# The attention loop of a hybrid encoder layer: single operations at written-down places instead of the automatic order

## Chip, cores and metric

The kernel runs on one core of one Trainium2 chip. The metric is the device time of one launch in microseconds (us), the median of the runs shown below. TensorE is called PE here, VectorE DVE, ScalarE ACT, GpSimd POOL and SyncE SP, as in the profile.

## What is computed

One encoder layer over 1024 rows of width 1024, in float32. The part that matters here is the windowed attention, the output projection behind it, and the router of the expert layer:

```
proj  = layer_norm(x) @ w_in                      # split into retention, S5 and attention columns
scores = q . k - slope * |t - s|                  # 8 heads, 2 key heads; a block of 128 rows sees 3 blocks of keys
m     = max(max(scores), sink)
p     = exp(scores - m);  denom = sum(p) + exp(sink - m)
y_att = (p / denom) @ v
mix   = concat(y_ret, y_ssm, y_att) @ w_out
h     = LN(alpha * h + mix)
aff   = softmax(h @ router_w)                     # 16 experts; each takes its 128 best rows
h     = LN(alpha * h + experts(h))                # SwiGLU, 16 experts of 1024 x 2048
```

## The kernel before

The 1024 rows are cut into 8 tiles of 128 rows (NT = 8, the last is LT = 7). The program has three stages. The first (`front`, up to about 284 us) makes the projections, the retention and S5 parts, and the scores of the first tile. The second, the attention loop (284 to about 460 us), is what the change is about; it ends in `last_tile`, which ranks the rows for the first expert. The third stage runs the experts, and lasts until 1604 us.

Most float32 products are made from a high part and a low part, each held in a type with a shorter mantissa: ACT copies the high part, DVE subtracts it from the value to get the low part, and PE multiplies the pairs (`mm3` issues three matmuls: L64, L65, L66 in the profile). So most tiles come as `xh`/`xl`, or as `[:, 0]` and `[:, 1]`.

The loop runs over i = 2 * tile + key head, 16 turns, and calls for each turn, with offsets between them:

- `attention_queries` (L1299): POOL starts the transfer of the queries of one turn, tile `qs`, three buffers.
- `attention_scores`: per head two matmuls into `at` (L1337, L1338), then one DVE instruction (L1341) that adds the bias, writes the scores `S` and gives the row maximum. Behind the four heads, two small DVE instructions (L1346, L1347).
- `attention_exp`: ACT takes exp of the four heads and their sums (L1357, L1359).
- `attention_out`: DVE adds and inverts the sums (L1369, L1370); ACT scales the four heads (L1372); for each of the 3 key blocks PE transposes four 128x128 blocks into `tp` (L1378), ACT and DVE split them into `pT` (L55, L56), and PE multiplies by the values into `po` (L1385). Then ACT and DVE split the result into rows of `yh`, `yl` (L55, L56, L1391).
- `out_proj_load`: the transfer of the old rows `z`, and the split of the retention and S5 rows into `yh`, `yl` (L55, L56).
- `out_proj_part`: 24 matmuls for one half of the columns (L64, L65, L66 into `mm`), then DVE adds them into `z` (L1425) and takes statistics (L1428). `out_proj_stats` finishes the statistics (L1436, L1438 on DVE, L1439 on POOL).
- `router`: PE transposes the new rows (L1478), ACT copies them (`rt`, L1480), PE multiplies by the router's weights (L1490), DVE and ACT make the softmax (`affinities`, L1498 to L1507); DVE normalizes `z` (L1512, L1517); SP stores the rows, ACT scales them, SP stores them again.
- `token_parts` (POOL) and `rank_tile`: a transpose of one column (L1610), ACT's copy (L1635), and DVE's counts (L1618, L1621; for tiles 2 and 5 also L1629).

Each engine works through one list of instructions in order. In `front` and `last_tile` the lists are written by hand (`tc.manual_schedule`). In the loop they are not: it stands outside of any such block, and a scheduler with a timeline of its own picks the order of the single instructions on each engine. Its order may mix the instructions of several calls and turns.

Of the kernel before, what the change touches and what calls it, by code (L numbers as in the profile page):

```python
# [945 lines left out]
def front(K, I, pool, close):  # L946
# [158 lines left out]
    def states_space():  # L1105
        close(X["c_s5a"], X["c_work"])
        X["ast"] = pool("ast")
        K.ast = X["ast"][1]
        X["s5v"] = pool("s5v")
        K.s5v = X["s5v"][1]  # L1110
        K.VS = K.s5v.tile([P, 2, 16, 16, 8], F32, name="VS")
        K.qscale = K.ast.tile([P, 4], F32, name="qscale")
        for u in range(4):
            for b in range(2):
                nc.gpsimd.memset(K.qscale[b * 64:(b + 1) * 64, u:u + 1], 2.0 ** (2 * u + b + 1) / 8.0)
        X["lags"] = Lags(K, I)
        level(K.ast, 160)
# [157 lines left out]
    for g, i, g0 in ((2.7, 0, 0), (9.5, 0, 2), (11.4, 1, 0), (13.5, 1, 2)):  # L1275
        at(A + g, lambda i=i, g0=g0: attention_scores(K, i, g0, g0 + 2))
# [3 lines left out]
    for g, i, g0 in ((10.4, 0, 0), (13.7, 0, 2), (15.65, 1, 0), (17.35, 1, 2)):  # L1280
        at(A + g, lambda i=i, g0=g0: attention_exp(K, i, g0, g0 + 2))
# [20 lines left out]
def attention_space(K):  # L1302
# [3 lines left out]
    K.heads = 0  # L1306
# [15 lines left out]
def attention_scores(K, i, g0=0, g1=4):  # L1322

    nc = K.nc
    c, kv = divmod(i, 2)
    b0, b1 = max(c - 1, 0), min(c + 2, NT)
    W, ro, k0 = (b1 - b0) * P, (b0 - c + 1) * P, b0 * P
    if g0 == 0:
        K.P[i] = [], K.small.tile([P, 5, 4], F32, name="asm", bufs=3)
    S, sm = K.P[i]  # L1330
    qs = K.Q[i]
    m, nm, rs, es, rd = (sm[:, k] for k in range(5))
    hs = slice(kv * 4, kv * 4 + 4)
    for g in range(g0, g1):
        h = kv * 4 + g
        ps = K.pat.tile([P, 512], F32, name="at")
        nc.tensor.matmul(ps[:, :W], qs[:, g, :], K.KHL[kv][:, 0, k0:k0 + W], start=True, stop=False)  # L1337
        nc.tensor.matmul(ps[:, :W], qs[:, g, :], K.KHL[kv][:, 1, k0:k0 + W], start=False, stop=True)  # L1338
        s = K.score[K.heads % 10]
        K.heads += 1  # L1340
        nc.vector.tensor_tensor_reduce(s[:, :W], ps[:, :W], K.R[:, ro:ro + W], 2.0 ** -(h + 1),  # L1341
                                       K.sink[:, h:h + 1], OP.add, OP.max, accum_out=m[:, g:g + 1])
        S.append(s)
    if g1 == 4:
        K.Q.pop(i)
        nc.vector.tensor_scalar(nm, m, -1.0, None, op0=OP.mult)  # L1346
        nc.vector.tensor_tensor(es, K.sink[:, hs], m, OP.subtract)  # L1347


def attention_exp(K, i, g0=0, g1=4):  # L1350
    nc = K.nc
    c = i // 2
    W = (min(c + 2, NT) - max(c - 1, 0)) * P
    S, sm = K.P[i]
    m, nm, rs, es, rd = (sm[:, k] for k in range(5))
    if g0 == 0:
        nc.scalar.activation(es, es, AF.Exp)  # L1357
    for g in range(g0, g1):
        nc.scalar.activation(S[g][:, :W], S[g][:, :W], AF.Exp, bias=nm[:, g:g + 1], accum_out=rs[:, g:g + 1])  # L1359


def attention_out(K, i):
    nc = K.nc
    c, kv = divmod(i, 2)
    b0, b1 = max(c - 1, 0), min(c + 2, NT)
    W = (b1 - b0) * P
    S, sm = K.P.pop(i)
    m, nm, rs, es, rd = (sm[:, k] for k in range(5))
    nc.vector.tensor_tensor(rd, rs, es, OP.add)  # L1369
    nc.vector.reciprocal(rd, rd)  # L1370
    for g in range(4):
        nc.scalar.activation(S[g][:, :W], S[g][:, :W], AF.Copy, scale=rd[:, g:g + 1])  # L1372
    po = K.po.tile([P, 512], F32, name="po")
    pTs = []
    for b in range(b0, b1):
        pt = K.ptp.tile([P, 4, P], F32, name="tp")
        for g in range(4):
            nc.tensor.transpose(pt[:, g, :], S[g][:, (b - b0) * P:(b - b0 + 1) * P], K.ident)  # L1378
        pT = K.ast.tile([P, 2, 512], F32R, name="pT", tag="k4", bufs=3)
        split(K, pT[:, 0], pT[:, 1], pt.rearrange("p a b -> p (a b)"))  # L1380
        pTs.append(pT)
    for b in range(b0, b1):
        pT = pTs[b - b0]
        for s in range(2):
            nc.tensor.matmul(po, K.AV[:, b, kv].rearrange("p s c -> p (s c)"), pT[:, s], start=(b == b0 and s == 0),  # L1385
                             stop=(b == b1 - 1 and s == 1))
    yh, yl, _ = K.Y[c]
    r = slice(kv * 64, (kv + 1) * 64)
    hi, lo = (po[i * 64:(i + 1) * 64].rearrange("p (a b) -> p a b", a=4) for i in range(2))
    split(K, yh[r, 4:8, :], yl[r, 4:8, :], hi)  # L1390
    nc.vector.tensor_tensor(yl[r, 4:8, :], lo, yl[r, 4:8, :].bitcast(F32), OP.add)  # L1391
# [8 lines left out]
def out_proj_load(K, t):  # L1400
    nc, pool, y = K.nc, K.op, K.y.pop(t)
    z = pool.tile([P, D], F32, name="z", bufs=3)
    rows = nc.sync.dma_start(z, K.h_dram[t])
    yh = K.opy.tile([P, KC, P], F32R, name="yh", bufs=2)
    yl = K.opy.tile([P, KC, P], F32R, name="yl", bufs=2)
    split(K, yh[:, 0:2, :], yl[:, 0:2, :], y)
    split(K, yh[:, 2:4, :], yl[:, 2:4, :], K.YO[:, :, t * 16:(t + 1) * 16, :].rearrange("p m k i -> p m (k i)"))
    K.Y[t] = yh, yl, z
    if t + 2 < NT:
        out_proj_rows(K, t + 2)  # L1410
    return rows


def out_proj_part(K, t, n, c0=0, c1=KC):

    nc = K.nc
    yh, yl, z = K.Y[t]
    ns = slice(n * 512, (n + 1) * 512)
    if c0 == 0:
        K.ps = K.pmm.tile([P, 512], F32, name="mm")  # L1420
    for c in range(c0, c1):
        mm3(nc, K.ps, (yh[:, c], yl[:, c]), [K.WO[s][c // 4][:, c % 4, ns] for s in range(2)], c == 0, c == KC - 1)
    if c1 < KC:
        return
    nc.vector.scalar_tensor_tensor(z[:, ns], z[:, ns], ALPHA, K.ps, op0=OP.mult, op1=OP.add)  # L1425
# [67 lines left out]
def affinities(K, t):  # L1493
# [13 lines left out]
    nc.vector.tensor_scalar(K.aff[:, t, :], a, s[:, 2:3], None, op0=OP.mult)  # L1507
# [12 lines left out]
def out_proj_store(K, t):  # L1520

    nc, z = K.nc, K.Y[t][2]
    nc.sync.dma_start(K.h1_dram[t * P:(t + 1) * P, :], z)
    late = t >= NT - 2
    ah = K.op.tile([P, D], F32, name="ah", tag="z" if late else "rt", bufs=3 if late else 1)
    nc.scalar.activation(ah, z, AF.Copy, scale=ALPHA)
    nc.sync.dma_start(K.acc_dram[t * P:(t + 1) * P, :], ah)


def router(K, t):  # L1530

    for q in range(2):
        router_turn(K, t, q)
    for q in range(2):
        router_part(K, t, q)
    affinities(K, t)
    out_proj_gain(K, t)
    out_proj_shift(K, t)
    out_proj_store(K, t)

# [72 lines left out]

def rank_before(K, row, t, col, own):
# [18 lines left out]
def rank_tile(K, t):  # L1633
    own = K.rows[:, t * P:(t + 1) * P]
    K.nc.scalar.activation(own, rank_row(K, K.aff[:, t, 0:1]), AF.Copy)  # L1635
    G = rank_before(K, K.rows[:, 0:(t + 1) * P], t, 0, own)
# [6 lines left out]
    return G  # L1643

# [398 lines left out]
def last_tile(K, I, O, pool, close):  # L2043

    nc, X, t = K.nc, K.X, LT - 1
    for q in range(2):
        router_turn(K, t, q)
# [6 lines left out]
    out_proj_store(K, t)  # L2054
# [33 lines left out]
    out_proj_store(K, LT)  # L2088
# [149 lines left out]
def build(tc, nc, I, O):  # L2238
# [55 lines left out]
    K.P, K.Y = {}, {}  # L2294
# [3 lines left out]
    K.mr, K.st, K.pr = {}, {}, {}  # L2298
    ahead = 2
# [133 lines left out]
```

## Time and profile before

| what | value |
|---|---|
| median of 3 runs | 1606.16 us (1604.99 to 1610.3) |
| the profiled execution | 1606.46 us, of it 1604.7 us in the span |
| granted PE clock over the span | 0.998 |
| busy: PE, DVE, ACT, POOL | 1560.3, 1404.2, 1118.0, 191.8 us |
| first transpose of the loop (L1378) | 284.52 us after the span's start |
| second sum of tile 6's rows (L1425) | 452.28 us |

The times of the profile are counted from the span's start. A matmul's own duration reaches into the next one's, since matmuls are pipelined; what PE needs for a row of them is read from the distance of their starts. A read of an accumulator (READ_ACCUMULATOR) belongs to the instruction ahead of it.

### The profile page before, as it was taken

What the parts mean: (1) busy time and instruction counts of PE and PEld (TensorE: products, weight loads), DVE (VectorE), ACT (ScalarE), POOL (GpSimd) and SP (SyncE); (2) the same over time, 40 slices, a digit from 0 to 9 for tenths busy, and PEclk for the clock granted to TensorE, in tenths of its full rate; (3) what the DMA queues carried; (4) which work ended last, traced back from release to release, by engine and by line L of the source; (5) the groups of instructions that cost most, each with busy time, mean ns of one, the idle gap of its engine ahead of it and who ended that gap; (6) DMA issues with size and microseconds to landing.
All of it is one profiled execution on the core that took longest, in us unless ns stands there. A gap on an engine that the chain in (4) does not pass through costs nothing.

```text
span 1604.7 us, 21040 instructions
## 1 busy us (share of the span) xinstructions
PE 1560.3 (97%) x7680; PEld 1276.0 (80%) x7680; DVE 1404.2 (88%) x1738; ACT 1118.0 (70%) x1275; POOL 191.8 (12%) x238
## 2 busy tenths in 40 slices
PE   6999999999999999999999999999999999999997
PEld 4887888787776788888888888888888888888885
DVE  7986874788787989999899999989999999899996
ACT  4645465877644677777777777777878877787873
POOL 4001111101010010110101001000202112020121
PEclk9999999999999999999999999999999999999999
DMA  5555479324248999999999999999999999999993
GB/s 185 202 160 129 133 214 258 108 79 148 79 183 309 348 371 391 398 389 385 378 388 387 371 371 382 400 409 417 405 405 414 405 410 417 409 421 409 402 408 153
DMA packets 101242, 506.78 MB, mean 316 GB/s; under 512 B 12817, under 2 KB 25873, under 8 KB 50450
## 3 DMA queue, kind: packets, MB, share of 16 engines
q1 hardware_dynamic: 84834, 474.50, 76.1%
q0 software_dynamic: 16304, 30.94, 6.8%
q8 instruction: 60, 0.98, 0.2%
q14 instruction: 44, 0.36, 0.1%
HBM read 461.36 MB, written 42.99 MB: 314 GB/s over the span
## 4 chain that ended last, share of the span: by engine, by line
PE 67%; DVE 13%; DMA 10%; ACT 5%; issue 4%; POOL 1%; SPq 0%; POOLq 0%; DVEq 0%; ACTq 0%
PE gu L1852 31%; PE y L1852 16%; DMA wraw<-in_exp_w_down 5%; DVE whl L1921 5%; PE mm L66 4%; PE mm L64 4%; PE mm L65 4%; DMA wraw<-in_exp_w_gate 2%; PE tp L1835 2%; PE gu L1860 1%; ACT whl L1912 1%; DMA wraw<-in_exp_w_up 1%; ACT S L1359 1%; PE po L1385 1%; DVE pT L56 1%
## 5 line engine op out<-in xcount | busy, mean ns | idle before, releaser
L1921 DVE TENSOR_TENSOR whl<-wraw,whl 128x2048 fp32r<-128x2048 f32 x378 | 857.5, 2286 | 68.1 <-ACT whl L1912 66.1
L1912 ACT ACTIVATE whl<-wraw 128x2048 fp32r<-128x2048 f32 x378 | 724.1, 1919 | 236.7 <-PE gu L1852 66.7
L1852 PE MATMUL gu<-whl,xT 128*128 128x512 f32 x3000 | 712.0, 394 | 0.0
L1852 PEld LDWEIGHTS gu<-whl,xT 128*128 128x128 f32 x3000 | 555.1, 188 | 113.5
L1852 PE MATMUL y<-whl,hT 128*128 128x512 f32 x1536 | 359.5, 390 | 0.0
L1852 PEld LDWEIGHTS y<-whl,hT 128*128 128x128 f32 x1536 | 288.1, 188 | 60.2 <-issue 0.5
L1814 POOL DMA_INDIRECT xs<-h_d,index x15 | 30.0, 1999 | 454.5 <-PE y L1852 301.4
L55 ACT ACTIVATE hT<-tp 128x512 fp32r<-128x512 f32 x80 | 46.0, 584 | 37.5 <-PE tp L1835 25.5
L64 PE MATMUL mm<-hT,whl 128*128 128x512 f32 x160 | 65.4, 409 | 0.0
L66 PE MATMUL mm<-hT,whl 128*128 128x512 f32 x160 | 62.5, 391 | 0.0
L65 PE MATMUL mm<-hT,whl 128*128 128x512 f32 x160 | 62.5, 391 | 0.0
L64 PE MATMUL mm<-WO,yh 128*128 128x512 f32 x128 | 51.9, 405 | 5.8 <-ACT yh L55 5.8
L56 DVE TENSOR_TENSOR hT<-tp,hT 128x512 fp32r<-128x512 f32 x80 | 54.0, 682 | 2.9 <-ACT hT L55 2.8
L65 PE MATMUL mm<-WO,yh 128*128 128x512 f32 x128 | 50.3, 393 | 0.0
L66 PE MATMUL mm<-WO,yl 128*128 128x512 f32 x128 | 49.4, 396 | 0.0
L1964 DVE TENSOR_TENSOR hid<-hid,gu 128x512 f32<-128x512 f32 x64 | 43.5, 680 | 4.6 <-PE gu L1860 3.2
L64 PE MATMUL mm<-whl,hT 128*128 128x512 f32 (+1 forms) x128 | 46.2, 361 | 1.1 <-ACT hT L55 1.1
L66 PE MATMUL mm<-whl,hT 128*128 128x512 f32 (+1 forms) x128 | 43.9, 343 | 1.4 <-DVE hT L56 1.4
L65 PE MATMUL mm<-whl,hT 128*128 128x512 f32 (+1 forms) x128 | 43.6, 341 | 0.2 <-DVE whl L120 0.2
L1359 ACT ACTIVATE S<-S,asm 128x384 f32<-128x384 f32 (+1 forms) x64 | 36.9, 579 | 8.9 <-DVE asm L1346 8.9
L1835 PE MATMUL tp<-ident,hid 128*128 128x128 f32 x256 | 38.8, 274 | 4.4 <-DVE hid L1964 4.4
L1835 PEld LDWEIGHTS tp<-ident,hid 128*128 128x128 f32 x256 | 31.1, 140 | 15.0 <-DVE hid L1964 8.0
(433 smaller groups left out, 1796.9 us busy)
## 6 DMA issues: line engine op xcount, KB each, us to landing
wraw<-in_exp_w_down SPq DMA_DIRECT2D x128, 1024.0 KB, 8.2
wraw<-in_exp_w_gate SPq DMA_DIRECT2D x126, 1024.0 KB, 8.6
wraw<-in_exp_w_up SPq DMA_DIRECT2D x124, 1024.0 KB, 8.4
wraw<-in_w_in SPq DMA_DIRECT2D x8, 1024.0 KB, 6.7
x<-in_x SPq DMA_DIRECT2D x8, 512.0 KB, 4.4
h_d<-x SPq DMA_DIRECT2D x8, 512.0 KB, 3.1
q_d<-kst SPq DMA_DIRECT2D x32, 128.0 KB, 3.0
wraw<-in_w_out SPq DMA_DIRECT2D x4, 1024.0 KB, 7.7
```

The lines of the kernel that those rows point to most:

```text
L55: nc.scalar.activation(hi, src, AF.Copy)
L56: eng.tensor_tensor(lo, src, hi.bitcast(F32), OP.subtract)
L64: nc.tensor.matmul(ps, a[0], b[0], start=start, stop=False)
L65: nc.tensor.matmul(ps, a[0], b[1], start=False, stop=False)
L66: nc.tensor.matmul(ps, a[1], b[0], start=False, stop=stop)
L1359: nc.scalar.activation(S[g][:, :W], S[g][:, :W], AF.Exp, bias=nm[:, g:g + 1], accum_out=rs[:, g:g + 1])
L1814: K.nc.gpsimd.indirect_dma_start(out=xs, out_offset=None, in_=K.h1_dram, in_offset=bass.IndirectOffsetOnAxis(ap=K.index[:, e:e + 1], axis=0))
L1835: K.nc.tensor.transpose(pt[:, c, :], src[:, (c0 + c) * P:(c0 + c + 1) * P], K.ident)
L1852: nc.tensor.matmul(ps, a[s][c], u[:, t, i * w:(i + 1) * w], start=first and id(ps) not in began, stop=last and left[id(ps)] == 0)
L1912: self.K.nc.scalar.activation(u[:, 0, :], self.raw[k1].rearrange("p a b -> p (a b)"), AF.Copy)
L1921: self.K.nc.vector.tensor_tensor(u[:, 1, :], raw, u[:, 0, :].bitcast(F32), OP.subtract)
L1964: at(self.after, q, 3, lambda: nc.vector.tensor_tensor(self.h[q], self.h[q], self.pg[q][1], OP.mult))
```

## The change

The functions of the loop are cut into single steps, each with one or a few instructions of one engine, and each step gets a place, a number: that of its kind in a table, plus 22.0 times the tile's number. `attention_steps` collects all steps of all tiles, sorts them by place, and issues them in that order, in a block of manual schedule (the class `Plan` was there before, and `front` uses it). So the order on each engine is the same in every tile of the loop's middle. The operations and their operands stay as they were; the scores and exps of tile 0 stay in `front`, and the last tile's projection and the router of tile 6 in `last_tile`.

```diff
+PERIOD = 22.0
+PLACES = {
+        "RD": (-10.53, -2.12),
+        "TP": ((-6.99, -2.93, -3.36), (7.65, 5.82, 4.91)),
...
+def attention_steps(K, I):
+    F, X = Plan(), K.X
+    def at(c, kind, *idx, fn):
+        place = PLACES[kind]
+        for k in idx:
+            place = place[k]
+        F.at(PERIOD * c + place, fn)
...
+            for g in range(4):
+                if i > 1:
+                    at(c, "SC", kv, g, fn=lambda i=i, g=g: attention_score(K, i, g))
+                    at(c, "SM", kv, g, fn=lambda i=i, g=g: attention_max(K, i, g))
+                    at(c, "EX", kv, g, fn=lambda i=i, g=g: attention_exp(K, i, g))
+                at(c, "SL", kv, g, fn=lambda i=i, g=g: attention_scale(K, i, g))
...
+    for k in range(2):
+        F.at(PERIOD * 4 + PLACES["LD"] + 0.01, lambda k=k: X.load(k))
+    F.run()
...
-    for i in range(2 * NT + 1):
-        if ahead <= i < 2 * NT:
-            if i not in K.Q:
-                attention_queries(K, i)
-            attention_scores(K, i)
-            attention_exp(K, i)
-        t, n = divmod(i - 1, 2)
-        if 0 <= t < NT:
-            if n == 0:
-                rows = out_proj_load(K, t)
...
-            attention_out(K, i - 1)
...
+    hold = tc.manual_schedule(engines={T.PE, T.Activation, T.DVE, T.Pool, T.SP})
+    hold.__enter__()
+    attention_steps(K, I)
     close(c_yo, c_kv, c_hl0)
...
-        K.P[i] = [], K.small.tile([P, 5, 4], F32, name="asm", bufs=3)
+        K.P[i] = [], K.small.tile([P, 5, 4], F32, name="asm", bufs=4)
```

The names of the steps, with engine: Q queries (POOL), SC scores (PE), SM biased scores and maximum (DVE), NG two small ones behind it (DVE), ES and EX exp (ACT), RD the inverted sums (DVE), SL scaling (ACT), TP transposes (PE), TH and TL split (ACT, DVE), PV values (PE), YH, YL, YM the rows of y (ACT, DVE, DVE), YS and YT the split of the other rows (ACT, DVE), LD and YD transfers (SP), OP three matmuls of the projection (PE), ZA and BN its sum and statistics (DVE), ST and PW the end of the statistics (DVE, POOL), RT, RC, RP, AF, AE, AG the router (PE, ACT, PE, DVE, ACT, DVE), GN and SH the normalized rows (DVE), H1, AH, AD their stores (SP, ACT, SP), TK (POOL) and RK, RW, RB (PE, ACT, DVE) the ranking. A number pair such as PV(1, 2) is key head 1, key block 2.

On PE in a tile of the middle, around the scores of one key head (KHL_2764 and KHL_2765 are the keys of head 0 and 1, WO_2916 and WO_3012 the weights of the projection's first and second half of inputs): before, word for word,

```order
L1378 MATMUL tp<-ident,S 128x128 x4
L1337 MATMUL at<-KHL_2764,qs 128x384
L1338 MATMUL at<-KHL_2764,qs 128x384
L1337 MATMUL at<-KHL_2764,qs 128x384
L1338 MATMUL at<-KHL_2764,qs 128x384
L64 MATMUL mm<-WO_3012,yh 128x512
L65 MATMUL mm<-WO_3013,yh 128x512
```

and now, around those of key head 1:

```order
L1385 MATMUL tp<-ident,S 128x128 x4
L1334 MATMUL at<-KHL_2765,qs 128x384 x4
L64 MATMUL mm<-WO_2916,yh 128x512
L65 MATMUL mm<-WO_2917,yh 128x512
L66 MATMUL mm<-WO_2916,yl 128x512
L1385 MATMUL tp<-ident,S 128x128 x4
L64 MATMUL mm<-WO_2916,yh 128x512
L65 MATMUL mm<-WO_2917,yh 128x512
L66 MATMUL mm<-WO_2916,yl 128x512
L1334 MATMUL at<-KHL_2765,qs 128x384 x4
```

Before, the second half of the projection's inputs (the attention rows of the same tile) comes right behind the scores. Now the first half of the inputs, whose rows are made from retention and S5, stands between the pairs of scores.

On ACT in a tile of the middle, the exps and the scaling of one turn, before:

```order
L1359 ACTIVATE S,asm<-S,asm 128x384
L1357 ACTIVATE asm<-asm 128x4
L1359 ACTIVATE S,asm<-S,asm 128x384 x3
L55 ACTIVATE pT<-tp 128x512
L55 ACTIVATE yh<-po 64x512
L55 ACTIVATE pT<-tp 128x512
L1372 ACTIVATE S<-S,asm 128x384 x4
```

and now:

```order
L1390 ACTIVATE pT<-tp 128x512
L1364 ACTIVATE S,asm<-S,asm 128x384
L1358 ACTIVATE asm<-asm 128x4
L1364 ACTIVATE S,asm<-S,asm 128x384
L1390 ACTIVATE pT<-tp 128x512
L1364 ACTIVATE S,asm<-S,asm 128x384
L1571 ACTIVATE aff,rsm<-nl,rsm 128x16
L1364 ACTIVATE S,asm<-S,asm 128x384
L1377 ACTIVATE S<-S,asm 128x384 x4
L1415 ACTIVATE yh<-po 64x512
```

The split of a transposed block, which stood behind all four exps, now stands between them, and the rows of y behind the scaling.

On DVE at the loop's end, the counts of tile 5 and the normalized rows of tile 6, before:

```order
L1618 TENSOR_SCALAR G,cnt<-rows,aff 128x768
L1621 SCALAR_TENSOR_TENSOR junk,cnt<-rows,aff,upto 128x128
L1391 TENSOR_TENSOR yl<-po,yl 64x512
L1512 SCALAR_TENSOR_TENSOR z<-z,l1mv,g_3151 128x1024
L1629 TENSOR_SCALAR G,cnt<-rows,aff 128x384
L1517 SCALAR_TENSOR_TENSOR z<-z,l1rs,b_3152 128x1024
L1629 TENSOR_SCALAR G,cnt<-rows,aff 128x384
L1498 SCALAR_TENSOR_TENSOR nl<-rsum,l1mv,sm 128x16
```

and now:

```order
L1813 TENSOR_SCALAR G,cnt<-rows,aff 128x768
L1816 SCALAR_TENSOR_TENSOR junk,cnt<-rows,aff,upto 128x128
L1824 TENSOR_SCALAR G,cnt<-rows,aff 128x384 x3
L1824 TENSOR_SCALAR G,cnt<-rows,aff 128x256
L1824 TENSOR_SCALAR G,cnt<-rows,aff 128x128
L1591 SCALAR_TENSOR_TENSOR z<-z,l1mv,g_3151 128x1024
L1596 SCALAR_TENSOR_TENSOR z<-z,l1rs,b_3152 128x1024
L1561 SCALAR_TENSOR_TENSOR nl<-rsum,l1mv,sm 128x16
```

All of tile 5's counts now stand ahead of tile 6's rows.

More of the change, by code (lines that the diff above doesn't have):

```diff
@@ L1319, in attention_consts, with attention_span @@
     nc.sync.dma_start(K.sink, bcast(I["attn_sink"], 8))
-def attention_scores(K, i, g0=0, g1=4):
-    nc = K.nc
-    c, kv = divmod(i, 2)
+def attention_span(i):
+    c = i // 2
     b0, b1 = max(c - 1, 0), min(c + 2, NT)
-    W, ro, k0 = (b1 - b0) * P, (b0 - c + 1) * P, b0 * P
-    if g0 == 0:
-        K.P[i] = [], K.small.tile([P, 5, 4], F32, name="asm", bufs=3)
[L1330 to L1347, printed above, removed]
@@ L1350, in attention_exp @@
[L1350 to L1391, printed above, removed]
@@ new lines, in attention_span, with attention_score, attention_max @@
+    return c, b0, b1, (b1 - b0) * P
+def attention_score(K, i, g):
+    c, b0, _, W = attention_span(i)
+    k0, KHL = b0 * P, K.KHL[i % 2]
+    ps = K.at[i, g] = K.pat.tile([P, 512], F32, name="at")
+    for s in range(2):
+        K.nc.tensor.matmul(ps[:, :W], K.Q[i][:, g, :], KHL[:, s, k0:k0 + W], start=s == 0, stop=s == 1)
+def attention_max(K, i, g):
+    c, b0, _, W = attention_span(i)
+    if g == 0:
+        K.P[i] = [], K.small.tile([P, 5, 4], F32, name="asm", bufs=4)
+    S, sm = K.P[i]
+    ro, h = (b0 - c + 1) * P, i % 2 * 4 + g
+    S.append(K.score[(4 * i + g) % 10])
+    K.nc.vector.tensor_tensor_reduce(S[g][:, :W], K.at.pop((i, g))[:, :W], K.R[:, ro:ro + W], 2.0 ** -(h + 1),
+                                     K.sink[:, h:h + 1], OP.add, OP.max, accum_out=sm[:, 0, g:g + 1])
@@ new lines, in attention_sum, with attention_scale, attention_turn @@
+def attention_sum(K, i):
+    _, _, rs, es, rd = (K.P[i][1][:, k] for k in range(5))
+    K.nc.vector.tensor_tensor(rd, rs, es, OP.add)
+    K.nc.vector.reciprocal(rd, rd)
+def attention_scale(K, i, g):
+    W, (S, sm) = attention_span(i)[3], K.P[i]
+    K.nc.scalar.activation(S[g][:, :W], S[g][:, :W], AF.Copy, scale=sm[:, 4, g:g + 1])
+def attention_turn(K, i, b):
+    b0, S = attention_span(i)[1], K.P[i][0]
+    pt = K.pt[i, b] = K.ptp.tile([P, 4, P], F32, name="tp")
+    for g in range(4):
+        K.nc.tensor.transpose(pt[:, g, :], S[g][:, (b - b0) * P:(b - b0 + 1) * P], K.ident)
@@ new lines, in attention_high, with attention_low, attention_values @@
+def attention_high(K, i, b):
+    K.pT[i, b] = K.ast.tile([P, 2, 512], F32R, name="pT", tag="k4", bufs=3)
+    K.nc.scalar.activation(K.pT[i, b][:, 0], K.pt[i, b].rearrange("p a b -> p (a b)"), AF.Copy)
+def attention_low(K, i, b):
+    pT = K.pT[i, b]
+    K.nc.vector.tensor_tensor(pT[:, 1], K.pt.pop((i, b)).rearrange("p a b -> p (a b)"), pT[:, 0].bitcast(F32), OP.subtract)
+def attention_values(K, i, b):
+    _, b0, b1, _ = attention_span(i)
+    if b == b0:
+        K.av[i] = K.po.tile([P, 512], F32, name="po")
+    pT = K.pT.pop((i, b))
+    for s in range(2):
+        K.nc.tensor.matmul(K.av[i], K.AV[:, b, i % 2].rearrange("p s c -> p (s c)"), pT[:, s], start=(b == b0 and s == 0),
+                           stop=(b == b1 - 1 and s == 1))
@@ L1400, in out_proj_load @@
 def out_proj_load(K, t):
[L1401 to L1410, printed above, removed]
@@ L1411, in out_proj_load, with out_proj_split @@
-    return rows
+    K.Y[t] = [None, None, K.op.tile([P, D], F32, name="z", bufs=3)]
+    K.nc.sync.dma_start(K.Y[t][2], K.h_dram[t])
+def out_proj_split(K, t, j, low):
+    Y = K.Y[t]
+    if j == low == 0:
+        for s in range(2):
+            Y[s] = K.opy.tile([P, KC, P], F32R, name=("yh", "yl")[s], bufs=2)
+    src = K.YO[:, :, t * 16:(t + 1) * 16, :].rearrange("p m k i -> p m (k i)") if j else K.y[t]
+    hi, lo = (y[:, 2 * j:2 * j + 2, :] for y in Y[:2])
+    if low:
+        K.nc.vector.tensor_tensor(lo, src, hi.bitcast(F32), OP.subtract)
+    else:
+        K.nc.scalar.activation(hi, src, AF.Copy)
@@ L1520, in out_proj_store, with out_proj_scale @@
 def out_proj_store(K, t):
-    nc, z = K.nc, K.Y[t][2]
-    nc.sync.dma_start(K.h1_dram[t * P:(t + 1) * P, :], z)
+    K.nc.sync.dma_start(K.h1_dram[t * P:(t + 1) * P, :], K.Y[t][2])
+def out_proj_scale(K, t):
     late = t >= NT - 2
[L1525 to L1538, printed above, removed]
-    out_proj_store(K, t)
+    K.ah[t] = K.op.tile([P, D], F32, name="ah", tag="z" if late else "rt", bufs=3 if late else 1)
+    K.nc.scalar.activation(K.ah[t], K.Y[t][2], AF.Copy, scale=ALPHA)
@@ L1611, in rank_row, with rank_turn, rank_keep @@
     return pt[:, 0, :]
+def rank_turn(K, t):
+    K.rank[t] = rank_row(K, K.aff[:, t, 0:1])
+def rank_keep(K, t):
+    K.nc.scalar.activation(K.rows[:, t * P:(t + 1) * P], K.rank.pop(t), AF.Copy)
 def rank_before(K, row, t, col, own):
@@ L2059, in last_tile @@
     out_proj_part(K, LT, 0, 7, KC)
+    half(0)
     G = rank_tile(K, t)
@@ L2297, in build @@
         c_ast, c_early, c_kv, c_yo, c_opy = front(K, I, pool, close)
-    K.mr, K.st, K.pr = {}, {}, {}
-    ahead = 2
+    K.mr, K.st, K.pr, K.ps, K.pt, K.pT, K.av, K.rpt, K.soft, K.ah, K.rank = ({} for _ in range(11))
     c_op, K.op = pool("op")
```

238 lines of the change are left out of this document (179 added, 59 removed).

## The prediction

> **What bounds the loop now.** I looked first at the stretches from tile to tile. Their ends come from the chain of waits: the last split of a tile's attention rows (L1391) lies 24.25 us after that of the tile before.
>
> ```profile
> 371.35 0.70 DVE yl L1391
> 395.60 0.70 DVE yl L1391
> ```
>
> Then the busy time of the engines in such stretches. Columns: stretch, its length, PE, PE's weight loads, DVE, ACT, POOL, each with its instructions, then PE's granted clock, DMA share and GB/s. The first two rows are tiles 0 and 1, which have less work; the third is a tile of the loop's middle.
>
> ```profile
> 284.50:302.10 17.60, 15.87 (x85) 12.87 (x83) 14.16 (x39) 16.48 (x45) 2.97 (x9) 1.00 0.67 195
> 302.10:323.10 21.00, 20.40 (x102) 16.37 (x101) 15.38 (x43) 14.83 (x39) 2.09 (x3) 1.00 0.10 20
> 371.40:395.60 24.20, 22.86 (x126) 18.99 (x125) 20.03 (x57) 16.83 (x44) 3.28 (x8) 1.00 0.37 103
> ```
>
> No engine is full in the third row, and the clock is at 1.00, so a tile's 24.2 us is set by waits between engines. A busy PE of 22.86 overstates PE's need, since matmuls overlap. So I read PE's need from the distance of starts, in PE's timeline (start, duration, instruction, idle time ahead of it):
>
> ```profile
> 354.12 0.96 PE L1490 MATMUL sm<-rwg,rt 128*128 128x16 f32 x8
> 354.93 0.63 PE L1378 MATMUL tp<-ident,S 128*128 128x128 f32 x4
> ...
> 355.63 0.34 PE L1337 MATMUL at<-KHL,qs 128*128 128x384 f32 x1
> 355.81 0.34 PE L1338 MATMUL at<-KHL,qs 128*128 128x384 f32 x1
> 355.99 0.35 PE L1337 MATMUL at<-KHL,qs 128*128 128x384 f32 x1
> ...
> 363.66 0.39 PE L66 MATMUL mm<-WO,yl 128*128 128x512 f32 x1
> 363.89 0.60 PE L1378 MATMUL tp<-ident,S 128*128 128x128 f32 x4
> 364.25 1.17 PE L1385 MATMUL po<-pT,AV 128*128 128x512 f32 x4
> 365.26 0.28 PE L1610 MATMUL tp<-ident,aff 128*128 128x128 f32 x1
> ...
> 368.19 0.33 PE L1338 MATMUL at<-KHL,qs 128*128 128x384 f32 x1
> 369.83 0.50 PE L64 MATMUL mm<-WO,yh 128*128 128x512 f32 x1 [1.31 <-ACT yh L55]
> ```
>
> A projection matmul takes 0.23 (363.66 to 363.89), a pair of scores 0.36 (355.63 to 355.99), four transposes 0.36 (363.89 to 364.25), four value matmuls 1.01 (364.25 to 365.26), eight of the router 0.81 (354.12 to 354.93). A middle tile has 48 projection matmuls (11.0), 8 pairs of scores (2.9), 6 groups of transposes of S and 2 of z (2.9; I give those of z the same price), 12 value matmuls (3.0), 16 of the router (1.6) and one for the rank (0.1): 21.5 us. PE idles some 2.7 us in each tile. The last row shows the largest piece: the scores are done at 368.19, and the next thing in PE's order waits for the attention rows until 369.83. Why they are late is seen on DVE and ACT:
>
> ```profile
> 367.77 0.08 DVE L1341 DVE_READ_ACCUMULATOR2_ANT asm<- 128x1 f32 x1
> 368.59 0.57 ACT L55 ACTIVATE pT<-tp 128x512 fp32r<-128x512 f32 x1
> 368.71 0.16 DVE L1369 TENSOR_TENSOR asm<-asm 128x4 f32<-128x4 f32 x1 [0.86 <-ACT S L1359]
> 369.19 0.69 DVE L56 TENSOR_TENSOR pT<-tp,pT 128x512 fp32r<-128x512 f32 x1
> 369.19 0.59 ACT L55 ACTIVATE yh<-po 64x512 fp32r<-64x512 f32 x1
> ```
>
> ACT runs all four exps of a turn ahead of two splits that have been ready, DVE waits 0.86 for the sums, and then a convoy of splits runs while PE has nothing that is ready.
>
> **The change, part by part.** No operation is added or taken away; the cost is all in the order.
>
> *The middle.* The table spaces PE's steps within 22.0 us per tile so that they don't overlap at the prices above: 21.5 us of work in 22.0. I went through what each step needs. The scores wait for their DVE readers of two heads before (at least 1.6 us of room by place), the values for the low parts (at least 1.1), the projection's chunk 4 for YM (1.12, where a DVE split takes 0.69). The tight ones are SC to SM of head 0 (0.57), TP to TH (0.67), EX to RD (0.76) and RD to SL (0.45); a delay there pushes a DVE or ACT step whose PE reader stands a microsecond or more behind. What stood behind the scores, the attention half of the projection, now comes 1.1 us behind its rows, and the half that needs no attention fills the gap. DVE has 20.03 busy in 22.0, ACT 16.83: both fit. So I take 22.0 per tile, with 21.5 as its floor. A late step doesn't stretch every tile, since there are 0.5 us to catch up in.
>
> *The start.* The old order may put projection matmuls between any others; the new one is fixed. After two transposed blocks and four scores PE has to do the first projection step, for which DVE must first do the last two S5 gates, RD of turn 1 and both YT. ACT ends the last gate's function and DVE the gate in these rows:
>
> ```profile
> 285.73 0.69 ACT L836 ACTIVATE glu<-mm,hb 128x512 f32<-128x512 f32 x1
> 287.02 1.22 DVE L837 SCALAR_TENSOR_TENSOR YO<-glu,yT 128x512 f32<-128x512 f32 x1
> ```
>
> Now that gate can start at 286.4 and ends at 287.6; with YT, RD and YT (1.0 together) PE's step comes at 288.7, while PE is free at 285.7: 3.0 us. A second wait: PV(1,1) of tile 0 stands behind TL(1,1), which stands on DVE behind RD of the next turn, which needs four exps that start only after two YH and TH: 2.5 us. With 0.5 of small ones that makes 6.0 us of waiting, beside 14.2 us of PE work in this stretch (7 groups of transposes, 8 steps of three projection matmuls, 10 scores, 5 value steps, at the prices above and 0.04 for each change of kind): 20.2 us, where the old order took 17.6 for a little more. In the next stretch PE has two tiles' projections at hand, 16 steps (11.0), 6 groups and 2 of z (3.1), 8 scores (2.8), 6 value steps (2.8): 19.7 us, and following the operands I find no wait, so 19.7.
>
> *The end.* From place 146.3 on there are no more scores. PE's work up to the last projection step of tile 6 is 14 such steps (9.6), 6 groups (2.2), 2 value steps (1.0), the router (1.6) and a rank (0.1): 14.5, with 0.4 for the last scaling: 14.9 us.
>
> *The sum.* From the first transposes to tile 6's second sum (first row below): before 452.28 - 284.52 = 167.8. After: 20.2 + 19.7 for the start, then from place 44.05 to 146.3 102.3 at one us per place, then 14.9: 157.1. That is 10.7 less.
>
> ```profile
> 452.28 0.67 DVE L1425 SCALAR_TENSOR_TENSOR z<-z,mm 128x512 f32<-128x512 f32 x1
> 455.48 1.01 DVE L1618 TENSOR_SCALAR_CACHE_REDUCE G<-rows,aff 128x768 bf16<-128x768 f32 x1
> 458.73 0.60 DVE L1629 TENSOR_SCALAR_CACHE_REDUCE G<-rows,aff 128x384 bf16<-128x384 f32 x1
> 463.54 0.29 PE L1610 MATMUL tp<-ident,aff 128*128 128x128 f32 x1 [0.52 <-DVE aff L1507]
> ```
>
> Then DVE rules: PE's rank transpose of tile 6 waits for DVE, 11.3 us after that sum. Now all five late counts of tile 5, not one, stand ahead of tile 6's rows, but BN, ST and YM come in the same sequence; adding up DVE's steps I get 12.1, so 0.8 is given back. Behind that the order is the same, and every transfer of expert weights but two waits for buffers that this stage frees, so I carry the rest to the end in full: 10.7 - 0.8 = 9.9 us. The profiled execution took 1606.46 (span 1604.7 and 1.8 around it), 0.3 over the median; against the median: 1606.2 - 9.9 = 1596.3 us.
>
> SP's order (stores, then next rows) keeps its neighbours, and the two weight loads stand behind tile 4's rows as before: nothing. A fourth buffer for the small sums: nothing.
>
> **Rivals.**
>
> *The period stays above 22.6.* If the tight pairs come late in each tile by more than 0.5 us, it lands between 22.6 and 23.6: 0.6 to 1.6 times 4.65 tiles is 2.8 to 7.4 more, 1599.1 to 1603.7. For it: five pairs have under 0.8 us, and the table has a DVE step of 0.53 for counts that take 1.0 and more.
>
> *DVE becomes the bound.* Two rows of splits show what a fresh wait costs:
>
> ```profile
> 365.28 0.69 DVE L56 TENSOR_TENSOR pT<-tp,pT 128x512 fp32r<-128x512 f32 x1
> 365.88 0.16 DVE L1346 TENSOR_SCALAR asm<-asm 128x4 f32<-128x4 f32 x1
> ...
> 369.92 0.68 DVE L56 TENSOR_TENSOR yl<-po,yh 64x512 fp32r<-64x512 f32 x1
> ```
>
> The step behind 365.28 starts 0.60 later, that behind 369.19 (quoted above) 0.73 later, where the operand had only just come. If all 34 steps of DVE in a tile met fresh operands, 20.03 + 34 * 0.11 = 23.8 per tile: 8.4 more, 1604.7, no change. Against it: half of the steps have over 0.8 us of room. The Trainium skill, "VectorE: DVE Perf Modes", section "The DRAIN you can't avoid", says that a semaphore between two DVE operations costs nothing extra; by that this rival would cost nothing and the sum would stay at 1596.3. The two distances here, 0.60 and 0.73, don't agree with it.
>
> *Slower: the queries come late.* POOL asks for key head 1's queries 6.1 us (places 44.17 and 50.27) ahead of the first score that needs them, and all of PE stands behind that score. Transfers of queries and their median time to landing over the loop, and the one issued at 363.66 beside the expert weights:
>
> ```profile
> qs<-q_d POOLq DMA_DIRECT2D x14, 256.0 KB, 3.3
> ...
> qs<-q_d POOLq DMA_DIRECT2D x1, 256.0 KB, 9.5
> ```
>
> At 9.5 each of five tiles would wait 3.4: 17 us, 1613. It undoes the gain from 8.1 us to landing on. The median of 3.3 speaks against it; the expert loads stand at place 74.0, 14 ahead of the next such request.
>
> *PE packs tighter.* PE's loads are busy only 18.99 of 24.20, and DVE with 20.03 is the fullest; if PE's matmuls close up to that, a tile takes about 21.0 and the time is 1591.6. Against it: the distances of starts were read where PE waited for nothing. The Trainium skill, "Perfetto Trace Analysis", section "Identifying the Most-Contended Engine", takes weight-load busy time, not matmul busy time, as PE's measure, and would put DVE first; by it this rival's 1591.6 would be the sum.
>
> *The gain isn't carried.* If the expert weights, not the loop, set the start of the third stage: 1606. Only two of the loads are issued before the loop's end.
>
> **Chances.** Forecast (period 21.6 to 22.6, 1594 to 1599.5) 0.58; longer period 0.20; DVE 0.07; late queries 0.06; tighter PE 0.05; not carried 0.04. A measurement of this kernel tells about 0.3%, 4.8 us, from no change: 1601.3. Of the longer period 0.12 lies below that, and 0.01 of the rest: faster 0.76, same 0.17, slower 0.07. The range takes in tighter PE and nearly all of the longer period: 1591 to 1603.
>
> **What would show it.** The distance of a tile's last splits: 22.0 (right), above 22.6 or below 21.5 (wrong). PE's wait of 1.3 behind the scores gone. A start that is 2 to 3 us longer. The distance from tile 6's second sum to its rank transpose: 12.1. From there to the end the same time as before. What would make it wrong: a wait that repeats in each tile and that I didn't see.

## The result and the profile after

| what | before | after |
|---|---|---|
| median of the runs | 1606.14 us (11 runs) | 1598.28 us (11 runs, 1595.78 to 1601.61) |
| ratio | 1 | 0.9944 (95%: 0.9928 to 0.9960), 9.0 us less (6.4 to 11.6) |
| the profiled execution | 1606.46, span 1604.7 | 1595.84, span 1594.1 |
| first transposes to tile 6's second sum | 167.76 us | 157.22 us |
| from there to tile 6's rank transpose | 11.26 us | 11.93 us |
| from there to the end | 1141.2 us | 1140.1 us |

Of the 10.6 us between the two profiled executions, 10.5 lie in the loop, as the fourth row shows.

The engines' busy time after, by stretch. The columns are as in the prediction: the stretch, its length, PE, PE's weight loads, DVE, ACT, POOL, PE's granted clock, DMA share, GB/s. The first row is the start, the third and fourth are tiles of the loop's middle.

```profile
284.87:302.22 17.35, 12.73 (x67) 9.74 (x66) 14.29 (x36) 14.78 (x41) 2.21 (x8) 1.00 0.66 190
302.22:324.75 22.53, 22.53 (x121) 19.29 (x120) 17.63 (x50) 17.09 (x43) 1.64 (x3) 1.00 0.07 12
324.75:346.73 21.98, 21.98 (x125) 19.04 (x125) 18.81 (x50) 16.37 (x41) 2.05 (x4) 1.00 0.36 103
346.73:368.84 22.11, 22.11 (x127) 19.10 (x126) 19.36 (x54) 16.64 (x42) 2.05 (x4) 1.00 0.59 197
```

From 302.22 on PE is busy in the whole of each stretch (to 442.20 the view shows it for every tile), where before it had 22.86 of 24.20. A tile lasts 22.1 us. At the start PE is idle for 4.6 of 17.35 us.

The last splits of two tiles' attention rows, in DVE's timeline, and what PE does around them:

```profile
340.79 0.69 DVE L1419 TENSOR_TENSOR yl<-po,yl 64x512 fp32r<-64x512 f32 x1
362.90 0.69 DVE L1419 TENSOR_TENSOR yl<-po,yl 64x512 fp32r<-64x512 f32 x1
...
362.41 0.95 PE L1334 MATMUL at<-KHL,qs 128*128 128x384 f32 x4
363.20 0.60 PE L1534 MATMUL tp<-ident,z 128*128 128x128 f32 x4
363.55 0.48 PE L64 MATMUL mm<-WO,yh 128*128 128x512 f32 x1
...
364.80 0.39 PE L66 MATMUL mm<-WO,yl 128*128 128x512 f32 x1
```

The distance is 22.11 (24.25 before). The split ends at 363.59, and the first matmul that reads it (L66 at 364.80) starts 1.2 us later. The wait of 1.31 behind the scores is gone: between them and this reader stand the router's transposes and a projection step that needs no attention.

The start and the end of the loop, in the timelines of PE and DVE:

```profile
286.67 0.40 PE L65 MATMUL mm<-WO,yh 128*128 128x512 f32 x1
289.54 0.50 PE L66 MATMUL mm<-WO,yl 128*128 128x512 f32 x1 [2.47 <-DVE yl L1458]
...
295.64 0.47 PE L1405 MATMUL po<-pT,AV 128*128 128x512 f32 x1 [0.80 <-DVE yl L1419]
297.00 0.96 PE L1405 MATMUL po<-pT,AV 128*128 128x512 f32 x3 [0.89 <-DVE pT L1395]
...
442.10 0.69 DVE L1476 SCALAR_TENSOR_TENSOR z<-z,mm 128x512 f32<-128x512 f32 x1 [0.73 <-PE mm L66]
...
449.37 1.28 DVE L1591 SCALAR_TENSOR_TENSOR z<-z,l1mv,g 128x1024 f32<-128x1024 f32 x1
...
454.03 0.29 PE L1797 MATMUL tp<-ident,aff 128*128 128x128 f32 x1 [2.02 <-DVE aff L1577]
```

The first projection step waits 2.5 us for the low part of tile 0's rows. The values of key head 1 wait first for DVE's split of the rows of key head 0 (0.80), then for the low part of a block (0.89). At the end DVE is busy for 10.5 of the 11.8 us from tile 6's second sum to the rank transpose, with the five late counts in between, and PE waits 2.0 us for it (0.5 before).

### The profile page after: what moved, and what is told of

It reads as the page before. It is cut to its first block, busy times and chain, and to the rows that moved or that the text cites. A ratio compares the mean times of both kernels' runs of the same rounds, so it can differ in the third digit from the quotient of the medians.

```text
span 1594.1 us, 21018 instructions
## 1 busy us (share of the span) xinstructions
PE 1556.4 (98%) x7680; PEld 1278.1 (80%) x7680; DVE 1406.8 (88%) x1738; ACT 1117.3 (70%) x1275; POOL 196.1 (12%) x238
## 4 chain that ended last, share of the span: by engine, by line
PE 69%; DVE 11%; DMA 10%; ACT 4%; issue 4%; POOL 1%; SPq 0%; POOLq 0%; ACTq 0%; DVEq 0%
PE gu L2051 30%; PE y L2051 15%; DVE whl L2120 5%; DMA wraw<-in_exp_w_down 5%; PE mm L64 4%; PE mm L66 4%; PE mm L65 4%; DMA wraw<-in_exp_w_gate 2%; ACT whl L2111 2%; PE tp L2034 2%; PE gu L2059 1%; PE po L1405 1%; PE tp L1385 1%; PE at L1334 1%; DVE hT L56 1%
## 5 line engine op out<-in xcount | busy, mean ns | idle before, releaser
L66 PE MATMUL mm<-hT,whl 128*128 128x512 f32 x160 | 62.5, 391 | 0.0
L66 PE MATMUL mm<-WO,yl 128*128 128x512 f32 x128 | 50.6, 396 | 2.5 <-DVE yl L1458 2.5
L66 PE MATMUL mm<-whl,hT 128*128 128x512 f32 (+1 forms) x128 | 44.4, 347 | 1.4 <-DVE hT L56 1.4
L2157 ACT ACTIVATE hid<-gu 128x512 f32<-128x512 f32 x64 | 37.2, 581 | 4.0 <-PE gu L2059 2.8
```

Source lines behind the costliest of these rows:

```text
L66: nc.tensor.matmul(ps, a[1], b[0], start=False, stop=stop)
L2157: nc.scalar.activation(self.h[q], self.pg[q][0], AF.Silu)
```

## Experiments

Each kernel is the changed one with the edit shown. "The stretch" is always that from the first transposes to tile 6's second sum (157.22 us after the change), "the period" the distance of a tile's first transposes from those of the tile before (22.1). Ratios are to the kernel before on the same chip. Theory A: in the loop's middle PE is the bound, and the places take its waits away.

### Single steps without places (auto)

```diff
-    hold = tc.manual_schedule(engines={T.PE, T.Activation, T.DVE, T.Pool, T.SP})
-    hold.__enter__()
     attention_steps(K, I)
+    hold = tc.manual_schedule(engines={T.PE, T.Activation, T.DVE, T.Pool, T.SP})
+    hold.__enter__()
```

> The single steps stay, and are issued in the same sequence, but outside of the block of manual schedule: the automatic scheduler picks each engine's order again. Theory A (the places carry the gain): the stretch from the first transposes to tile 6's second sum goes back from 157.2 us to 163 to 169, the time to within 5 us of before. Rival (cutting the functions into single steps is enough, since it frees the scheduler): that stretch is at most 159 us and the time at most 2 us over the changed kernel's.

The stretch was 163.9 us, the ratio 1.0016 (1.0000 to 1.0031). Two periods, and PE's longest wait in the second:

```profile
350.53:374.54 24.01, 22.76 (x128) 19.14 (x126) 19.36 (x54) 16.67 (x44) 3.26 (x8) 1.00 0.36 102
374.54:398.54 24.00, 22.75 (x128) 19.13 (x127) 19.46 (x54) 16.63 (x44) 3.26 (x8) 1.00 0.33 94
...
397.06 0.50 PE L64 MATMUL mm<-WO,yh 128*128 128x512 f32 x1 [1.25 <-ACT yh L1415]
```

The scheduler, given the same single steps in the table's sequence, comes back to 24.0 us per tile with the old wait for the attention rows. The places carry the gain: the cut into steps alone makes the stretch 3.8 us shorter, not 10.5, and the time shows nothing of that.

### PE's old neighbour, ACT's old neighbour (half_first, exps_first)

The first moves two steps on PE alone (the places of YH, YL, YM and BN change so that their engines' orders stay), the second four steps on ACT alone.

```diff
-  "OP": ((1.86, 8.08, 14.31, 16.57, 17.25, 17.94, 20.20, 20.89), ...
+  "OP": ((1.86, 8.08, 14.31, 16.57, 14.306, 14.307, 20.20, 20.89), ...
```

```diff
-  "ES": (-13.41, -6.37),
-  "EX": ((-12.23, -13.31, -11.29, -14.01), ...
+  "ES": (-14.55, -6.37),
+  "EX": ((-14.53, -14.54, -14.52, -14.56), ...
```

> On PE alone the first two projection steps that need the attention rows (chunks 4 and 5) stand right behind the last values again, ahead of chunk 2, the transposes, the scores and chunk 3; the orders of the other engines are the same. In the changed kernel's trace the values end at 361.36 and the rows of y at 363.59, so PE waits 1.8 us in each tile for them. Theory A (PE has no slack left): all of it is paid, 7 times 1.8 = 12.6 us more, the period 23.9 and the time about that of before or a little over. Rival (another engine sets the period and PE's wait is absorbed): at most 3 us more.

> On ACT alone the four exps of key head 0 stand together again ahead of the two splits, as in the kernel before; the orders of the other engines are the same. Theory A (PE is the bound, and behind these splits its readers stand over a microsecond later): by the trace the splits come 2 to 3 us later, DVE's steps behind them 1.0, PE's readers just in time: 0 to 0.3 us per tile, 0 to 2 us in all. Rival (the row of exps on ACT was the cause of PE's wait before): 1.0 to 1.3 per tile, 7 to 9 us.

With the two projection steps ahead, the period is 24.86 (2.8 more), the stretch 179.3 (22.0 more), the ratio 1.0064 (1.0040 to 1.0088). PE's timeline in one tile, all rows with a listed wait:

```profile
382.53 0.66 PE L1534 MATMUL tp<-ident,z 128*128 128x128 f32 x4 [0.59 <-DVE pT L1395]
397.73 0.50 PE L64 MATMUL mm<-WO,yh 128*128 128x512 f32 x1 [0.68 <-ACT yh L1415]
399.18 0.50 PE L66 MATMUL mm<-WO,yl 128*128 128x512 f32 x1 [0.72 <-DVE yl L1419]
```

The last two waits are the 1.8 us that I had worked out (0.85 and 0.9 by the distances of starts). The first is another: the router's transposes wait for a `tp` buffer, which the split of a transposed block (L1395) frees, and that block's transposes now start behind the wait. So a wait of 1.8 on the bound engine cost 2.8, since it delayed work that PE itself waits for later. The rival is out; theory A holds, though it had the price too low (12.6 us in all). Of the 22.0 us, 5.3 lie ahead of the seventh group of transposes, where PE's clock was at half twice (last section); the price of the order itself is read from the period.

With the exps in a row on ACT, the stretch was 156.75, the period 22.09, the ratio 0.9948 (0.9930 to 0.9966): no cost. ACT's two splits come 2.5 and 1.2 us later in the tile (at 378.74 and 379.23, in a row behind the exps), and PE's readers still come behind them. So PE's neighbour decides: with the old one PE waits though the exps are spread, with the new one it doesn't though they stand in a row. How much the row of exps added to the wait of the kernel before isn't shown, since no run changes it under the old order of PE.

### What PE and DVE have to spare (less_pe, dve1, dve2)

```diff
     for c in range(c0, c1):
+        if t < LT and c in (1, 2, 3):
+            for s in range(2):
+                K.nc.tensor.matmul(K.ps[t, n], yh[:, c], K.WO[s][c // 4][:, c % 4, n * 512:(n + 1) * 512],
+                                   start=False, stop=False)
+            continue
```

```diff
-            at(c, "BN", n, fn=lambda c=c, n=n: out_proj_half(K, c, n))
+            for _ in range(2):
+                at(c, "BN", n, fn=lambda c=c, n=n: out_proj_half(K, c, n))
```

(In dve2 it is `range(3)`.)

> Left out: the third matmul (low part of the rows) of chunks 1 to 3 in both halves of the projection of tiles 0 to 6, six matmuls or 6 * 0.2325 = 1.4 us of PE per tile; all orders stay. Theory A (PE alone is the bound): the period goes from 22.1 to 20.7 to 20.9, 8 to 10 us less in all. Rival (DVE, 19.4 busy with its waits, or the chain scores, exps, sums, scaling, transposes binds as well): 0 to 3 us less.

> Each of the two statistics steps of the projection (one DVE instruction of 0.69 us that nothing on PE waits for soon) is issued twice, to the same result: 1.38 us more of DVE per tile, 19.4 to 20.8 in a period of 22.1. Theory A (PE is the bound and DVE has 2.6 us to spare per tile): the stretch from the first transposes to tile 6's second sum grows by 0 to 2 us. Rival (DVE's order is nearly tight, since it waits for fresh operands in between): 0.5 to 1.4 per tile, 4 to 10 us.

> The same steps are issued three times: 2.76 us more of DVE per tile, 22.2 busy where the period was 22.1. Theory A: now DVE is the bound, the period is 22.2 plus the 0.5 to 1.5 us that DVE still waits for fresh operands, 22.7 to 23.7, and the stretch grows by 4 to 12 us. Rival (PE waits for few of DVE's steps and buffers give room, so that it is absorbed): 0 to 2 us.

One period of each, in that order, and a second of dve2:

```profile
367.88:388.56 20.68, 20.68 (x121) 17.97 (x120) 19.43 (x54) 16.64 (x43) 4.93 (x8) 1.00 0.38 109
...
367.81:389.89 22.08, 22.08 (x127) 19.07 (x126) 20.65 (x56) 16.64 (x44) 4.93 (x8) 1.00 0.36 102
...
366.43:389.02 22.59, 22.47 (x128) 18.94 (x127) 21.88 (x58) 16.68 (x43) 5.04 (x8) 1.00 0.35 100
389.02:412.52 23.50, 22.39 (x127) 18.76 (x126) 22.75 (x64) 16.94 (x44) 3.35 (x7) 1.00 0.28 84
```

1.4 us less of PE make the period 1.41 shorter, with PE still busy throughout; 1.38 us more of DVE make no difference to it; 2.76 more make four tiles 22.2, 22.5, 22.6 and 23.5, where theory A said 22.7 to 23.7, with DVE busy for all but 0.7 to 1.1 us of each. So PE is the bound at 22.1, DVE follows close behind (busy for 20.65 it costs nothing, busy for 21.88 half a microsecond), and at 20.7 nothing else binds yet. The stretches were 150.0, 158.9 and 161.6; that of less_pe is 7.2 shorter, not 8 to 10, as the start has waits that aren't PE's work (and a time at half clock, below). That of dve1 is 1.7 longer; it too has a time at half clock at the start, as the run again below, whose stretch is 1.1 longer with no more work. Ratios: 0.9933 (0.9912 to 0.9955), 0.9963 (0.9942 to 0.9983), 0.9991 (0.9975 to 1.0008).

### The start (head, head2)

```diff
+FIRST = {("YT", 0): -3.30, ("OP", 0, 0): 1.86, ("OP", 0, 1): 1.87,
+         ("OP", 1, 0): 1.88, ("OP", 1, 1): 1.89,
+         ("OP", 0, 2): 13.30, ("OP", 1, 2): 13.31, ("OP", 0, 3): 13.32}
...
+        if c == 0:
+            place = FIRST.get((kind, *idx), place)
```

head2 has besides `("YS", 1): -1.75, ("YT", 1): -0.50, ("OP", 1, 3): 15.00`, and `("OP", 0, 2)` at 8.08.

> Tile 0 alone has other places: the low part of its first rows is made ahead of the last two S5 gates on DVE, and seven of its projection steps stand where PE waited 2.6, 2.0 and 0.9 us in the first 17 us (four behind the first scores, three ahead of key head 1's values). Theory A (PE is the bound from here on, so what fills its waits is gained): of 6.0 us of waiting some 2 stay, the stretch from the first transposes to tile 6's second sum goes from 157.2 to 152.5 to 154.5, the time 3 to 4.5 us less. Rival (at the start DVE, 14.3 of 17.4 busy, and its chain set the pace): 0 to 1 us less.

> As in the kernel with other places for tile 0, and besides: the split of the S5 rows stands behind the splits of the first transposed blocks on ACT and DVE, one projection step between the scores of key head 1, and one ahead of tile 1's first transposes. There 3.6 us of PE's waiting were left, 1.0 for score buffers, 1.6 for the low parts of the first blocks, 0.5 for tile 1's scaling. Theory A (each wait that is filled is gained): 2 of these 3.6 go, and the stretch is 153 to 154.5 us where it was 155.4; the time 3 to 5 us under the changed kernel's. Rival (DVE, with the gates ahead of it, is the bound of this start): 155 us and no gain over the kernel before it.

The stretch was 155.4 in the first, 1.8 less: half of what theory A said, since four projection steps filled the first wait and then the low parts of the first blocks were late (3.6 of the 6.0 us by distances of starts stayed). In the second it was 153.7, as expected. Its two first stretches, which correspond to the first 17.35 and the next 19.85 us of the changed kernel, and PE's longest wait there (one more is over 0.3 us, 0.41 ahead of 304.21):

```profile
284.65:300.64 15.99, 15.20 (x79) 11.90 (x78) 13.71 (x36) 14.55 (x40) 2.21 (x8) 1.00 0.70 206
300.64:318.36 17.72, 17.32 (x95) 14.49 (x94) 15.82 (x43) 14.62 (x40) 0.75 (x1) 1.00 0.08 16
...
295.61 0.95 PE L1405 MATMUL po<-pT,AV 128*128 128x512 f32 x3 [0.55 <-DVE pT L1395]
```

Ratios: 0.9926 (0.9903 to 0.9949) and 0.9932 (0.9917 to 0.9948; median 1593.77). The changed kernel, run beside head2, had 0.9967 (0.9954 to 0.9979), so head2 is 5.5 us faster by the medians there (3 to 5 were expected). Its median is the lowest of all that ran; its ratio isn't told apart from those of head and less_pe.

### The late counts (tail)

```diff
-    if t == 5:
-        for a in range(5):
-            rank_after(K, a, max(a + 1, 3), 6, 3)
...
     affinities(K, t)
+    rank_late(K)
...
-    half(0)
     G = rank_tile(K, t)
+    half(0)
```

(`rank_late` holds the five counts.)

> The five late counts of tile 5 (2.85 us of DVE) stand behind tile 6's softmax instead of ahead of its normalized rows, and the sum and statistics of tile 7's first half behind tile 6's own counts. If DVE alone sets this stretch, the way from tile 6's second sum to its rank transpose goes from 11.9 to 9.8 us, where PE's projection steps are the next bound; the gather of the candidates starts 1.5 to 2 us earlier, and the time is 1.5 us less. Rival (the counts only move: DVE does the same work before the gather): the transpose comes 2 us earlier but the gather and the end 0 to 0.5 us.

The transposes came 9.75 us behind the sum instead of 11.93, as worked out. The numbers of the candidates (which the gather needs) were ready 16.8 us behind the sum instead of 17.6, which is 0.8 earlier and not 1.5 to 2, and the end came 1153.2 behind it instead of 1152.0. In the profiles of the kernels that leave this part alone the last distance lies between 1151.6 and 1154.7, so the end shows neither gain nor loss within 3 us, which agrees with the rival; one profile can't tell 0.5 from 1.5 there. Ratio 0.9940 (0.9918 to 0.9963).

### The same once more, and three buffers (again, asm3)

```diff
-        K.P[i] = [], K.small.tile([P, 5, 4], F32, name="asm", bufs=4)
+        K.P[i] = [], K.small.tile([P, 5, 4], F32, name="asm", bufs=3)
```

> The changed kernel once more, beside the next one on the same chip: 0.994 of before, a stretch from the first transposes to tile 6's second sum of 157 to 158 us with a period of 22.1. The start of the stretch is expected at 284.9 or, where the last weights of the projection land late and PE waits 2.9 us for the split behind them, 4 to 5 us later, since four of eight other profiles showed the one and four the other.

> The small sums have three buffers again instead of four. From the scores to the last scaling of a turn the places span 18.2 us, three turns 33 us. Theory (as predicted, the fourth buffer is worth nothing): the period stays 22.1, the stretch 157 to 158. Rival (three are not enough for this order): a first reduction that waits for the scaling of three turns before, 0.5 us or more per tile.

Three buffers: period 21.96, stretch 157.6, no wait for them; the fourth is worth nothing. The ratio was 0.9969 (0.9950 to 0.9987), with a start 5.7 us later than in the first profile (below). The changed kernel again: 0.9967, median 1599.25 against 1605.27, which is 5.3 us (3.4 to 7.4), less than the first 9.0 and less than I expected; stretch 158.3, period 22.1, the stretch's start at 286.1.

## Why the prediction was right

Forecast was 1596.3 us, within 1591 to 1603, and faster; measured 1598.28, 0.9944 of before.

- *The middle.* 22.0 per tile was forecast; 22.1 came, with PE full. Beyond the 21.5 us of its work, PE idles 0.6 us per tile where it idled 2.7. The tight pairs (rival "the period stays above 22.6") are late by little and PE's readers stand behind them. From place 44.05 to 146.3 it took 101.7 us (forecast 102.3).
- *The start.* Forecast 20.2 and 19.7; to the ends of the same steps it took 20.4 and 19.8. Less the 14.2 of PE's work, 6.2 of the 20.4 are waiting (6.0 forecast). By the distances of starts it is 2.6 and 2.1 at the two places that I named (3.0 and 2.5 forecast), and the small ones come to 1.5, not 0.5. Ahead of the second, PE also waits for DVE's split of key head 0's rows, which I hadn't listed, but the low part comes later still. "A start that is 2 to 3 us longer" holds for the same work: 20.4 where the old order took 17.6. Counted to the seventh group of transposes it doesn't show (17.35 against 17.1), since the old order had done more of the projection by then.
- *The end of the loop.* 14.9 forecast, 15.4 measured; the sum of all 157.1, measured 157.2. That the sum is nearer than its parts is luck: the start is 0.3 over the forecast, the middle 0.6 under it, the end 0.5 over it.
- *Given back.* 12.1 forecast from the second sum to the rank transpose, 11.93 measured. The run with the late counts moved shows that they are the cause, and that without them PE's steps bound it at 9.8. That it counts to the end isn't shown: moving them brought nothing there that stands out of the scatter, and from tile 6's second sum to the end it was 1152.5 us before and 1152.0 after.
- *Carried to the end.* 1141.2 before, 1140.1 after. Over the profiles of all kernels it is 1137.9 to 1142.7 (1143.5 in tail, whose transpose itself comes 2.2 us earlier), with no relation to the stretch, so the carry is in full within that scatter.
- *DVE becomes the bound* was priced at 23.8 per tile by 0.11 for each fresh operand. dve2 shows 21.9 busy in 22.6 and 22.75 in 23.5: the waits between DVE's steps come to 0.7 in these tiles, not 3.7. The larger of the two distances it was made from, 0.73, was no distance between two DVE steps alone: the step at 369.92 reads what ACT wrote until 369.78 (369.19 and 0.59). The rule in the Trainium skill, "VectorE: DVE Perf Modes", section "The DRAIN you can't avoid", that a semaphore between two DVE operations costs nothing extra, is nearer to that than my price was, and the two distances don't speak against it.
- *PE packs tighter* (21.0) is refuted: 1.38 more of DVE cost nothing and 1.40 less of PE gave 1.41. Weight-load busy time, which the Trainium skill, "Perfetto Trace Analysis", section "Identifying the Most-Contended Engine", names beside the share of peak flops as PE's measure, puts DVE (19.4) ahead of PE (19.1) here; by itself it doesn't find the bound in this case.
- *The queries* landed 3.1 to 3.7 us from issue in the loop's middle; PE waited for none.
- *The cause of the old wait.* I put the lateness of the rows on ACT's row of exps and the convoy behind it, and the gain on work that is ready in the gap. exps_first shows that the row of exps costs nothing with the new order on PE, and half_first that with the old step next on PE the wait is back though the exps are spread. So the gain rests on what stands next on PE; the part of the exps in the old wait stays open.

One thing the steps don't give. The medians fell by 7.9 us in the first comparison, and by 6.0 in the second, while the stretch fell by 10.5 and 9.4 in the profiles. One part of that is in the last section: the new order brings two waits on PE behind which its clock can fall. The granted clock over the span, as a mean of the runs, was 0.9959 for the kernel before, 0.9948 for the changed one beside it, and 0.9962 for head2, which is without the first of the two waits; 0.0011 of 1596 us are 1.8 us of clock lost. Whether the rest is more than scatter isn't shown, since each kernel has one profile, and the runs of the changed kernel differ by 6 us, those of the kernel before by 11.

## What to carry to other kernels

Before an order is written by hand, add up the bound engine's instructions by the distances of their starts, in a stretch where it waits for nothing: that sum (21.5 here) is the least that a fixed order can take, and the order written for 22.0 ran at 22.1. On that engine put the step whose operand comes last a microsecond behind it, and fill the gap with work that has been ready for long; the other engines' order may then be loose by one or two microseconds. A loop's first pass needs places of its own, because its operands come from elsewhere: that was worth another 3.5 us in the stretch. And a wait on the bound engine can cost its clock besides (next section).

## What the runs showed of the hardware

PE's granted clock falls to half behind times in which PE is little busy. In nine profiles PE waits 2.46 to 2.48 us ahead of the first low part (L66); in six of them (half_first, less_pe, dve1, tail, again, asm3) the clock is 0.50 soon after, for 3.41 us (in half_first for 6.83, and later once more for 3.41), in three (after, exps_first, dve2) it stays at 1.00. The four profiles without that wait (before, auto, head, head2) show no drop there. The clock's record in the traces tells why the same wait gives the one or the other: in each profile all changes of the clock lie a multiple of 3.41 us apart, on a grid whose place differs between executions. Again and after, each cut at its own grid:

```profile
288.95:292.37 3.42, 1.10 (x4) 0.60 (x5) 2.90 (x8) 3.02 (x7) 0.70 (x6) 1.00 0.97 166
292.37:295.78 3.41, 3.41 (x14) 3.11 (x13) 1.61 (x8) 1.87 (x4) 0.00 (x0) 0.50 0.97 335
...
285.06:288.48 3.42, 2.01 (x14) 1.57 (x12) 2.38 (x3) 2.27 (x8) 1.31 (x7) 1.00 0.01 1
288.48:291.89 3.41, 1.89 (x9) 1.33 (x10) 3.34 (x12) 2.55 (x7) 0.13 (x1) 1.00 1.21 243
291.89:295.30 3.41, 2.95 (x17) 2.16 (x15) 2.99 (x9) 3.41 (x11) 0.16 (x1) 1.00 0.89 342
```

In again most of the wait falls into one interval of the grid, in which PE is busy for 1.10 us, and the next interval has half the clock. In after the wait is shared by two intervals, with 2.01 and 1.89 busy, and the clock stays. Over all 13 profiles, from 30 us after the start to 12 us before the end, 18 intervals at full clock had PE busy for 0.45 of their length or less (0.007 to 0.452), and each was followed by one at half clock; no interval at full clock with 0.459 or more was. So here it took some 1.9 us of idle time within 3.41 us, and where the grid lay decided. The stretch is 1.1 us longer in again than in after.

The wait of 2.0 us for the rank transpose, which the new order makes longer too, is a second such place: the clock fell behind it in half_first, less_pe, dve1, dve2, head2 and asm3, and not in after, exps_first, head and again. From tile 6's second sum to the end it took 1153.1 to 1154.7 us with that drop and 1151.6 to 1153.8 without (dve1 and dve2, which have more to do there, left out). In tail, where PE waits at most 1.2 us there, the clock stays.

The Trainium skill, "TensorE: Matmul & The Clock Gate", section "What's actually happening", tells of a free-running window of about 3.4 us, and of half the clock after an idle one; the grid of 3.41 us agrees, but the intervals here weren't wholly idle. Its section "HAM oscillation — how this bites in real kernels" gives gaps of over 3.4 us as the limit; here 2.5 us were enough.

The second finding lies ahead of the loop, in code that the change doesn't touch. The stretch starts between 284.5 and 290.6 us. Where the last weights of the projection land late, ACT waits for them with the split, the S5 step behind it on ACT is late, and PE waits (in less_pe: 2.9 us, in asm3 3.75):

```profile
276.18 2.00 ACT L910 ACTIVATE WO<-wraw 128x1024 fp32r<-128x1024 f32 x2 [2.30 <-DMA wraw<-in_w_out]
278.09 0.58 ACT L812 ACTIVATE YG<-mm 128x512 f32<-128x512 f32 x1
...
278.72 1.95 PE L820 MATMUL tp<-ident,YG 128*128 128x128 f32 x8 [2.88 <-ACT YG L812]
```

In all five profiles with such a wait of over 2 us (auto, less_pe, head, tail, asm3) the clock fell behind it too, to 0.5, and the loop began 4 to 6 us later than in the earliest. That is as much as the runs of the changed kernel differ.
